# MLP's second projection: half of its work on columns 0 to 1023 as seven block products with 15 sums, in place of eight

## The chip, the cores and the metric

The kernel runs on one core of one Trainium2 chip. The metric is device time in microseconds (us), the median of several runs of one launch. A core has five engines, each with its own instruction stream: TensorE (PE: matmuls, and PEld for its weight loads), VectorE (DVE), ScalarE (ACT), GpSimd (POOL) and SyncE (SP), which here issues nearly all DMAs. Matmul results land in PSUM, which has 8 banks of 128 x 512 f32; everything else lives in SBUF.

## The reference

One layer of a streaming encoder on 256 tokens of width 2048, all in f32: a mixer (retention and gated delta rule), a cross-attention into 256 memory tokens, a squared-ReLU MLP and a final norm. What matters here is the last part:

```python
D_MODEL = 2048
SEQ = 256
D_FF = 4 * D_MODEL
...
        h = rms_norm(x, norm_ffn_g[l])
        x = x + jnp.square(jax.nn.relu(h @ w_ff1[l])) @ w_ff2[l]
    return rms_norm(x, norm_final_g)
```

`w_ff1` is 2048 x 8192 and `w_ff2` 8192 x 2048, 64 MB each.

## The kernel before

**Three matmuls for one product.** Each f32 operand is split into a rounded part ("hi", type fp32r) and the remainder ("lo"). A product is hi x hi + hi x lo + lo x hi: three matmuls into one PSUM bank.

**How a weight arrives.** `fetch` (L94) loads 512 x 512 weights (1 MB) by one DMA into a `raw` tile of 128 x 2048, of which there are three. It cuts it into two halves of 128 x 1024. For each half ScalarE rounds it into a `whi` tile (L117), and VectorE takes the remainder into a `wlo` tile (L118). `whi` and `wlo` have three buffers each, so a half can be made ready when TensorE has finished the half three before it.

**The MLP.** The hidden width is worked in four quarters (`fb`, 2048 hidden rows each). In a quarter the first projection runs first: eight calls of `blocks` (L183), each of which makes 256 hidden rows for all 256 tokens with hidden rows on the partitions. `evac_h` squares the ReLU into `hs` (two 128-row blocks of 256 tokens) and splits it into `hid`, four quads of four 128-row blocks, hi and lo. Then the second projection runs over four column blocks of 512 (`n`), one call of `chunk` (L145) each: it fetches the four 512-row pieces `q` of the quarter's weights for these columns and adds 16 row blocks x 2 token halves x 3 matmuls of 512 columns into two banks, one per half of the tokens (`t`). `evac_o` adds each bank, times the row's squared norm factor, into the residual `res` (L1125). In the last quarter it also sums the squares and multiplies by the final gain; the very last chunk has its own evacuation (`evac_last`) and keeps half of its weights in a space of its own (`hold`), so that the end is short.

**Banks.** `stream_ps` hands out a pair of banks (`s0`, `s1`) of which there are two pairs; `bank` hands out one of four others (`b`).

**Order.** The order of each engine's instructions is fixed when the program is built, by a planner that takes what is ready by a priority: the place in the program, moved ahead by 100000 places for a fetch with its rounding (`high_priority(offset=100000)`) and by 50000 for the evacuations. On the chip each engine then keeps to this order and waits where an operand or a buffer is late.

**Around the MLP.** `rt` (128 x 16 x 256) holds the residual in feature order until VectorE has transposed it blockwise into `tr`, of the same size (L1094). During the first projection of quarter 0, `place` (L1096) moves `tr` into the token-order residual `res` by 32 DMAs of 64 KB on SP. After that neither `rt` nor `tr` is used.

Of the kernel before, what the change touches and what calls it, by code (L numbers as in the profile page):

```python
# [10 lines left out]
F32 = mybir.dt.float32  # L11
F32R = mybir.dt.float32r
# [40 lines left out]
def trunk(ctx: ExitStack, tc: tile.TileContext, x_f, mem_f, positions, lead_f, small_f, w_in, ret_gn_g, w_out, w_xq,  # L53
# [213 lines left out]
    def square_sum(acc, src):  # L267
        junk = sm.tile([P, 512], F32, name="junk", tag="junk", bufs=1)
        act.activation(junk[:, :src.shape[1]], src, AF.Square, accum_out=acc)
# [831 lines left out]
                nc.sync.dma_start(to, tr[32 * a:32 * a + 32, :, b8 * 32:b8 * 32 + 32])  # L1101

    ssq4 = cp.tile([P, NT, 5], F32, name="ssq4")
    for fb in range(4):
        hid = []
        for b2 in range(8):
            hs = fp.tile([P, 2, S], F32, name="hs", tag="hs", bufs=2)
            if b2 % 2 == 0:
                hid.append(quad_a())

            def evac_h(b, ps):
                vec.scalar_tensor_tensor(hs[:, b, :], ps, 0.0, ps, op0=ALU.max, op1=ALU.mult)  # L1112
                qh, ql = (a[:, b2 % 2 * 2 + b, :] for a in hid[-1])
                act.activation(qh, hs[:, b, :], AF.Copy)
                vec.tensor_sub(ql, hs[:, b, :], qh.bitcast(F32))  # L1115

            blocks(h3, w_ff1[0], fb * D + b2 * 256, 2, evac_h)
            if fb == 0:
                place(b2)
        for n in range(4):  # L1120
            ns = slice(n * 512, (n + 1) * 512)

            def add(t, ps, c0, c1):
                got = res[:, t, n * 512 + c0:n * 512 + c1]
                vec.scalar_tensor_tensor(got, ps, rstd3q[:, t:t + 1], got, op0=ALU.mult, op1=ALU.add)  # L1125
                return got

            def evac_o(t, ps, c0, c1):
                got = add(t, ps, 0, 512)
                if fb == 3:  # L1130
                    square_sum(ssq4[:, t, n:n + 1], got)
                    vec.tensor_mul(got, got, gfin[:, ns])

            def evac_last(t, ps, c0, c1):
                got = add(t, ps, c0, c1)
                acc = ssq4[:, t, 4 if c0 else 3:5 if c0 else 4]
                if t == 0:
                    square_sum(acc, got)
# [16 lines left out]
                for c in (0, 3, 1, 2):  # L1155
# [7 lines left out]
                        act.activation(o, o, AF.Copy, scale=r)  # L1163
                    (act if t and c in (3, 2) else nc.sync).dma_start(out[0, t * P:(t + 1) * P, cs], o)

            last = fb == 3 and n == 3
            sums = []
            chunk(hid, cols(w_ff2[0, fb * D:(fb + 1) * D, :], n * 512), evac_last if last else evac_o,
                  hold=quad_b if last else None)


# [40 lines left out]
```

## Time and profile before

| | |
|---|---|
| time, median of 3 runs | 2066.89 us (2066.78 to 2068.17) |
| the profiled execution's own time | 2066.57 us |
| its span (first to last instruction) | 2064.8 us |
| granted TensorE clock, mean | 0.999 |
| DMA | 405.24 MB, mean 196 GB/s |
| MLP in the span | about 1360 to 2054 us |

The profile is of one execution, on the hardware. A page has busy times by engine, a chain of waits followed back from the last instruction, and groups of instructions by line and shape ("out<-in, partitions x elements"), with the mean duration and the idle time of the engine just before them and what ended it. Other views give the waits by pair, the instructions in order of time, or the busy time in chosen stretches. TensorE's matmuls overlap and their ends are modelled, so its busy time doesn't give its rate; the distance between starts does.

### The profile page before, as it was taken

Reading aid. Unit: us, or ns where it says so; the run is one execution under the profiler, and the core shown is the slowest. Engines: PE = TensorE matmul, PEld = TensorE weight load, DVE = VectorE, ACT = ScalarE, POOL = GpSimd, SP = SyncE. Lnnn points to the kernel's source line nnn. Section 1 sums busy time; section 2 is a strip of 40 time slices with the busy share of each in tenths; the row PEclk is TensorE's granted clock in tenths of the full one; section 3 lists DMA queues with packets and bytes.
Section 4 is the critical chain, followed back from the end, with each engine's and each line's share of the span. In section 5 each row is a group of like instructions: output and inputs, shape, how many; then the busy total and the mean of one; then the engine's idle time right before and its main releaser. Section 6 shows DMA issues by size and latency. Waiting matters only on the chain.

```text
span 2064.8 us, 28349 instructions
## 1 busy us (share of the span) xinstructions
PE 2054.2 (99%) x10922; PEld 1769.7 (86%) x10922; DVE 1412.2 (68%) x2249; ACT 1096.4 (53%) x1787; POOL 37.4 (2%) x50
## 2 busy tenths in 40 slices
PE   9999999999999999999999999999999999999998
PEld 7888888988888888888888898888888888888887
DVE  5887788778667975887567665776556556655655
ACT  5655764575457555755455555554344434434444
POOL 0000000000000000000000000000000000000000
PEclk9999999999999999999999999999999999999999
DMA  9689556565555655565577664678566566656654
GB/s 326 205 256 301 183 186 195 157 193 187 175 184 184 190 191 165 180 195 177 163 228 226 188 183 136 202 203 231 199 188 194 189 194 193 187 201 186 197 189 143
DMA packets 329224, 405.24 MB, mean 196 GB/s; under 512 B 34928, under 2 KB 239360, under 8 KB 328960
## 3 DMA queue, kind: packets, MB, share of 16 engines
q1 hardware_dynamic: 328656, 402.74, 62.4%
q8 instruction: 85, 1.39, 0.3%
q10 hardware_dynamic: 432, 0.69, 0.1%
q14 instruction: 51, 0.42, 0.1%
HBM read 389.74 MB, written 11.55 MB: 194 GB/s over the span
## 4 chain that ended last, share of the span: by engine, by line
PE 98%; DMA 1%; DVE 0%; issue 0%; ACT 0%; SPq 0%; POOLq 0%; POOL 0%; ACTq 0%; DVEq 0%
PE s L200 34%; PE s L201 18%; PE s L159 13%; PE s L160 13%; PE s L158 13%; DMA raw<-w_xkv 1%; PE b L779 1%; PE b L682 1%; PE b L130 1%; PE b L812 1%; PE b L129 1%; PE b L131 1%; PE s L385 0%; PE b L684 0%; PE s L386 0%; PE s L384 0%
## 5 line engine op out<-in xcount | busy, mean ns | idle before, releaser
L118 DVE TENSOR_TENSOR wlo<-raw,whi 128x1024 fp32r<-128x1024 f32 x696 | 850.7, 1223 | 493.3 <-ACT whi L117 484.0
L117 ACT ACTIVATE whi<-raw 128x1024 fp32r<-128x1024 f32 x696 | 737.4, 1060 | 701.3 <-PE s L160 355.6
L200 PE MATMUL s<-q,whi 128*128 128x512 f32 x3072 | 1059.1, 391 | 1.3 <-DVE q L126 1.3
L201 PE MATMUL s<-q,wlo 128*128 128x256 f32 x3072 | 836.8, 281 | 0.0
L200 PEld LDWEIGHTS s<-q,whi 128*128 128x128 f32 x3072 | 566.8, 188 | 112.4 <-DVE q L126 1.5
L201 PEld LDWEIGHTS s<-q,wlo 128*128 128x128 f32 x3072 | 576.9, 188 | 13.9 <-DVE wlo L118 0.4
L159 PE MATMUL s<-wlo,q 128*128 128x512 f32 (+1 forms) x1200 | 469.8, 391 | 0.0
L160 PE MATMUL s<-whi,q 128*128 128x512 f32 (+1 forms) x1200 | 467.4, 390 | 0.0
L158 PE MATMUL s<-whi,q 128*128 128x512 f32 (+1 forms) x1200 | 428.0, 390 | 0.0
L158 PEld LDWEIGHTS s<-whi,q 128*128 128x128 f32 x1200 | 225.2, 188 | 46.8
L160 PEld LDWEIGHTS s<-whi,q 128*128 128x128 f32 x1200 | 225.4, 188 | 45.7
L159 PEld LDWEIGHTS s<-wlo,q 128*128 128x128 f32 x1200 | 225.4, 188 | 45.4
L207 ACT ACTIVATE bo<-s 128x256 f32<-128x256 f32 x192 | 73.2, 381 | 112.9 <-PE s L201 112.8
L208 DVE TENSOR_TENSOR bo<-bo,s 128x256 f32<-128x256 f32 x192 | 80.0, 417 | 55.3 <-ACT bo L207 55.0
L641 DVE SCALAR_TENSOR_TENSOR acc<-bo,small,acc 128x255 f32<-128x255 f32 (+1 forms) x144 | 65.3, 480 | 1.8 <-ACT acc L638 0.6
L748 DVE TENSOR_TENSOR pr<-lw,tw 32x31 f32<-32x31 f32 (+15 forms) x124 | 40.4, 326 | 7.8 <-DMA lw<-scr_l 5.8
L750 DVE TENSOR_TENSOR tw<-tw,pr 32x31 f32<-32x31 f32 (+15 forms) x124 | 40.6, 328 | 2.1
L1125 DVE SCALAR_TENSOR_TENSOR res<-s,rstd3q,res 128x512 f32<-128x512 f32 (+1 forms) x32 | 22.3, 735 | 11.4 <-PE s L160 11.4
L638 ACT ACTIVATE acc<-bo,small 128x256 f32<-128x256 f32 x48 | 24.7, 514 | 7.7 <-DVE bo L208 7.6
L913 ACT ACTIVATE gth<-s 128x512 f32<-128x512 f32 x32 | 18.9, 590 | 16.8 <-PE s L160 12.6
L1112 DVE SCALAR_TENSOR_TENSOR hs<-bo 128x256 f32<-128x256 f32 x64 | 26.9, 422 | 1.1
L1115 DVE TENSOR_TENSOR q<-hs,q 128x256 fp32r<-128x256 f32 x64 | 26.7, 418 | 0.0
(309 smaller groups left out, 1170.7 us busy)
## 6 DMA issues: line engine op xcount, KB each, us to landing
raw<-w_in SPq DMA_DIRECT2D x143, 1024.0 KB
raw<-w_ff SPq DMA_DIRECT2D x128, 1024.0 KB
raw<-w_xkv SPq DMA_DIRECT2D x29, 1024.0 KB
raw<-w_out SPq DMA_DIRECT2D x16, 1024.0 KB
raw<-w_xq SPq DMA_DIRECT2D x16, 1024.0 KB
raw<-w_xo SPq DMA_DIRECT2D x16, 1024.0 KB
dec_d<-dec_w SPq DMA_DIRECT2D x8, 384.0 KB
dec<-dec_d SPq DMA_DIRECT2D x8, 384.0 KB
```

The source lines that it names most:

```text
L117: latest["hi"] = act.activation(hi[:, cs], src[:, cs], AF.Copy).ins
L118: latest["lo"] = vec.tensor_sub(lo[:, cs], src[:, cs], hi[:, cs].bitcast(F32)).ins
L158: pe.matmul(o, xh, wh, start=first, stop=False)
L159: pe.matmul(o, xh, wl, start=False, stop=False)
L160: pe.matmul(o, xl, wh, start=False, stop=last)
L200: pe.matmul(ps[b], lh, xhl, start=kk == 0, stop=False)
L201: pe.matmul(ps[b][:, :S], ll, xh, start=False, stop=kk == KT - 1)
L207: act.activation(o, ps[b][:, S:], AF.Copy)
L208: vec.tensor_add(o, o, ps[b][:, :S])
L641: vec.scalar_tensor_tensor(acc[:, d:], ps[:, :S - d], cw[:, j, blk:blk + 1], acc[:, d:], op0=ALU.mult, op1=ALU.add)
L748: vec.tensor_mul(pv, lw[:, j, j + 1:32].unsqueeze(2).to_broadcast([32, n, j + 1]), tw[:, j, 0:j + 1].unsqueeze(1).to_broadcast([32, n, j + ...
L750: vec.tensor_sub(tw[:, j + 1:32, 0:j + 1], tw[:, j + 1:32, 0:j + 1], pv)
```

## The change

Columns 0 to 1023 and the first 1024 hidden rows of each quarter are computed otherwise; the other 1024 rows of these columns, and columns 1024 to 2047, are computed as before. The hidden rows are taken as 128-row blocks in pairs, even and odd. With the token halves t0, t1 and the columns 0 to 511 and 512 to 1023 this makes a 2 x 2 block product: a11 and a12 are the even and odd hidden blocks of t0, a21 and a22 those of t1; b11 and b12 are the even weight blocks of the two column halves, b21 and b22 the odd ones. Eight block products become seven:

| product | goes to (column half, token half) |
|---|---|
| a11 b11 | `shared`, then (0, t0) |
| S1 (b12 - b11), S1 = a21 + a22 | `p5`, then (1, t0) and (1, t1) |
| S4 b22, S4 = a12 - S2 | the bank of (1, t0) |
| + S2 (b22 - b12 + b11), S2 = S1 - a11 | `shared` (on top of the first), then (1, t0) |
| a12 b21 | the bank of (0, t0) |
| + S3 (b22 - b12), S3 = a11 - a21 | `shared` (on top of both), then (0, t1) and (1, t1) |
| a22 (b21 - b22 + b12 - b11) | the bank of (0, t1) |

The four sums of the hidden are made and split by `token_sums`, called from `evac_h` for the first four of the eight blocks of the first projection. The four sums of the weights are made in place by VectorE in `form`, then rounded as a fetch is. The weight blocks are loaded by `load_block` into the spaces of `rt` and `tr`, 1 MB each. `seven` interleaves the products with the ordinary pieces (`plain`) of column blocks 2, 0 and 1, and uses all eight banks; column block 3 remains a `chunk`.

```diff
+    def add(n, t, ps, c0=0, c1=512):
+        got = res[:, t, n * 512 + c0:n * 512 + c1]
+        with tc.high_priority(offset=50000):
+            vec.scalar_tensor_tensor(got, ps, rstd3q[:, t:t + 1], got, op0=ALU.mult, op1=ALU.add)
+        return got
+
+    def finish_sum(n, t, ps, fb):
+        got = add(n, t, ps)
+        if fb == 3:
+            square_sum(ssq4[:, t, n:n + 1], got)
+            vec.tensor_mul(got, got, gfin[:, n * 512:(n + 1) * 512])
+
+    s_hl = tuple(fp.tile([P, 4, 512], F32R, name="s" + e, tag="s" + e, bufs=1) for e in "hl")
+    b11, b12, b22, b21 = (a[:, c:c + 8, :].rearrange("p k s -> p (k s)") for a in (rt, tr) for c in (0, 8))
+
+    def token_sums(i, hs):
+
+        sv = fp.tile([P, 4, P], F32, name="sv", tag="sv", bufs=1)
+        (a11, a21), (a12, a22) = ((hs[:, b, 0:P], hs[:, b, P:S]) for b in range(2))
+        vec.tensor_add(sv[:, 0], a21, a22)
+        vec.tensor_sub(sv[:, 1], sv[:, 0], a11)
+        vec.tensor_sub(sv[:, 2], a11, a21)
+        vec.tensor_sub(sv[:, 3], a12, sv[:, 1])
+        split([a[:, i, :] for a in s_hl], sv.rearrange("p a s -> p (a s)"))
+
+    def load_block(to, rows, which, n):
+
+        src = rows[0:D // 2, n * 512:(n + 1) * 512].rearrange("(i two p) n -> p i two n", two=2, p=P)[:, :, which, :]
+        with tc.high_priority(offset=100000):
+            fetched.append(nc.sync.dma_start(to.rearrange("p (i n) -> p i n", i=4), src).ins)
+
+    def seven(fb, hid, rows):
+
+
+        own = [stream_ps() for _ in range(2)]
+        shared, p5 = bank(), bank()
+        own.append([bank(), bank()])
+        opened = set()
+
+        def triple(o, lhs, rhs, last=False):
+            for j, (l, r) in enumerate(((0, 0), (0, 1), (1, 0))):
+                pe.matmul(o, lhs[l], rhs[r], start=id(o) not in opened, stop=last and j == 2, skip_group_check=True)
+                opened.add(id(o))
...
+        def form(raw, minus=None):
+            got = []
+            with tc.high_priority(offset=100000):
+                for c in range(2):
+                    src = raw[:, c * 1024:(c + 1) * 1024]
+                    if minus is not None:
+                        vec.tensor_sub(src, *(a[:, c * 1024:(c + 1) * 1024] for a in minus))
+                    hi, lo = (wp.tile([P, 1024 + room], F32R, name=nm, tag=nm, bufs=3)[:, :1024]
+                              for nm, room in (("whi", 64), ("wlo", 0)))
+                    latest["hi"] = act.activation(hi, src, AF.Copy).ins
+                    latest["lo"] = vec.tensor_sub(lo, src, hi.bitcast(F32)).ins
+                    got.append((hi.rearrange("p (k n) -> p k n", n=512), lo.rearrange("p (k n) -> p k n", n=512)))
+            return got
+
+        def product(o, lhs, halves, last=True):
+            for i in range(4):
+                triple(o, lhs(i), [a[:, i % 2, :] for a in halves[i // 2]], last=last and i == 3)
...
+        plain(2, 0)
+        load_block(b22, rows, 1, 1)
+        product(shared, part(0, 0), form(b11))
+        add(0, 0, shared)
+        plain(2, 1)
+        load_block(b21, rows, 1, 0)
+        product(p5, summed(0), form(b11, (b12, b11)))
+        add(1, 0, p5)
+        add(1, 1, p5)
+        plain(0, 2)
+        product(own[1][0], summed(3), form(b22), last=False)
+        plain(2, 2)
+        product(shared, summed(1), form(b11, (b22, b11)))
+        add(1, 0, shared)
+        plain(0, 3)
+        product(own[0][0], part(1, 0), form(b21), last=False)
+        finish_sum(0, 0, own[0][0], fb)
+        plain(2, 3)
+        for t in range(NT):
+            finish_sum(2, t, own[2][t], fb)
+        product(shared, summed(2), form(b12, (b22, b12)))
+        add(0, 1, shared)
+        add(1, 1, shared)
+        plain(1, 2)
+        product(own[0][1], part(1, 1), form(b11, (b21, b11)), last=False)
+        finish_sum(0, 1, own[0][1], fb)
+        plain(1, 3)
+        for t in range(NT):
+            finish_sum(1, t, own[1][t], fb)
+
     for fb in range(4):
         hid = []
+        rows = w_ff2[0, fb * D:(fb + 1) * D, :]
...
+                if b2 < 4 and b:
+                    token_sums(b2, hs)
 
             blocks(h3, w_ff1[0], fb * D + b2 * 256, 2, evac_h)
+            if b2 > 5:
+                load_block((b11, b12)[b2 - 6], rows, 0, b2 - 6)
             if fb == 0:
                 place(b2)
-        for n in range(4):
+        seven(fb, hid, rows)
+        for n in range(3, 4):
```

`plain(n, q)` fetches one 512 x 512 piece and runs its 24 matmuls into the two banks of column block `n`; `part` and `summed` pick the hidden block or the sum that is the stationary operand.

More of the change, by code (lines that the diff above doesn't have):

```diff
@@ L1164, in evac_last @@
                     (act if t and c in (3, 2) else nc.sync).dma_start(out[0, t * P:(t + 1) * P, cs], o)
-            last = fb == 3 and n == 3
+            last = fb == 3
             sums = []
-            chunk(hid, cols(w_ff2[0, fb * D:(fb + 1) * D, :], n * 512), evac_last if last else evac_o,
+            chunk(hid, cols(rows, n * 512), evac_last if last else evac_o,
                   hold=quad_b if last else None)
```

21 lines of the change are left out of this document (12 added, 9 removed).

## The prediction

> **What bounds the kernel now.** I read the page from the top: span and busy times, then the chain of waits, then the list of who waited for whom on TensorE.
>
> ```profile
> span 2064.8 us, 28349 instructions
> ...
> PE 2054.2 (99%) x10922; PEld 1769.7 (86%) x10922; DVE 1412.2 (68%) x2249; ACT 1096.4 (53%) x1787; POOL 37.4 (2%) x50
> ...
> PE 98%; DMA 1%; DVE 0%; issue 0%; ACT 0%; SPq 0%; POOLq 0%; POOL 0%; ACTq 0%; DVEq 0%
> ```
>
> ```profile
> PE s L200 <- DVE q L126: 1.3, 1, 1.3
> PE b L242 <- DVE warm L238: 1.1, 1, 1.1
> PE s L384 <- DVE q L319: 0.5, 1, 0.5
> PE s L385 <- DVE wlo L118: 0.2, 1, 0.2
> ```
>
> The second fence is TensorE's whole list of waits (total us, times, longest): 3.1 us in the kernel, none of them on the MLP's lines L158 to L160. So a matmul taken out there comes off the end, as long as TensorE goes on finding its operands ready. Busy time says little about that pace, since matmuls overlap; the pace has to come from when things start. In the second projection one half of a fetched weight (128x1024) feeds 12 matmuls of 512 columns, and ScalarE's next rounding is released when TensorE has finished a half:
>
> ```profile
> 1481.48 1.06 ACT L117 ACTIVATE whi<-raw 128x1024 fp32r<-128x1024 f32 x1 [1.66 <-PE s L160]
> 1484.20 1.06 ACT L117 ACTIVATE whi<-raw 128x1024 fp32r<-128x1024 f32 x1 [1.66 <-PE s L160]
> 1486.92 1.06 ACT L117 ACTIVATE whi<-raw 128x1024 fp32r<-128x1024 f32 x1 [1.66 <-PE s L160]
> ```
>
> ```profile
> 1486.43 1.40 DVE L1125 SCALAR_TENSOR_TENSOR res<-s,rstd3q,res 128x512 f32<-128x512 f32 x2
> 1488.01 1.23 DVE L118 TENSOR_TENSOR wlo<-raw,whi 128x1024 fp32r<-128x1024 f32 x1 [0.18 <-ACT whi L117]
> ```
>
> ```profile
> 1486.72 0.62 PE L158 MATMUL s<-whi,q 128*128 128x512 f32 x2
> ```
>
> The starts lie 2.72 us apart (1484.20 less 1481.48), so a matmul costs 2.72 / 12 = 0.2267 us. The last three rows give the price of making a half ready: TensorE goes on to the next half at 1486.72; the buffer of the finished one is rounded from 1486.92 and its remainder taken from 1488.01 to 1489.24. That is 2.52 us, for a buffer needed two halves (5.44 us) later: 2.9 us to spare. The three views of TensorE, ScalarE and VectorE agree that the two helpers wait for TensorE here.
>
> By stretches (columns: busy us of PE, PEld, DVE, ACT, POOL, then clock, DMA share, GB/s) a second projection is 1443 to 1530 or 1618 to 1705, and a first projection lies between:
>
> ```profile
> 1443.00:1530.00 87.00, 87.00 (x385) 72.04 (x385) 45.33 (x45) 35.11 (x36) 0.00 (x0) 1.00 0.60 194
> 1530.00:1618.00 88.00, 88.00 (x511) 77.90 (x510) 55.62 (x77) 42.00 (x60) 0.00 (x0) 1.00 0.63 191
> 1618.00:1705.00 87.00, 87.00 (x387) 72.05 (x386) 45.21 (x45) 35.11 (x36) 0.00 (x0) 1.00 0.60 193
> ```
>
> VectorE is half idle (45 of 87 us) where the change puts its sums, and the granted clock is 1.00.
>
> **What goes.** For columns 0 to 1023 and the first 1024 rows of each quarter, before has 2 column blocks x 2 fetches x 4 row blocks x 2 token halves x 3 matmuls = 96; after has 7 products x 4 x 3 = 84. Twelve fewer in each of four quarters: 48 x 0.2267 = 10.9 us. All are 128x512 forms, so the price needs no other row.
>
> The Trainium skill, "TensorE: Matmul & The Clock Gate", in the section on the 56 ns gap, puts a warm matmul at N / 2.4 GHz plus about 2.5 ns, 215.7 ns for 512 columns; by that the saving would be an estimated 10.4 us. Here the pace is 226.7 ns, and I keep the row.
>
> **What comes: rounding, sums and adds in the second projection.** The costs of one are in these groups (last columns: busy us, mean ns, then idle before):
>
> ```profile
> L118 DVE TENSOR_TENSOR wlo<-raw,whi 128x1024 fp32r<-128x1024 f32 x696 | 850.7, 1223 | 493.3 <-ACT whi L117 484.0
> L117 ACT ACTIVATE whi<-raw 128x1024 fp32r<-128x1024 f32 x696 | 737.4, 1060 | 701.3 <-PE s L160 355.6
> ```
>
> Per quarter, the seven products round 14 halves where there were 8 (6 more on ScalarE, 6 more on VectorE), four of the products form their weight operand with two 128x1024 differences each (8 more on VectorE, of the form and size of L118: 1.223 us), and 6 more results of 128x512 are added into the residual (0.70 each, two in 1.40). VectorE gets 14 x 1.223 + 6 x 0.70 = 21.3 us, ScalarE 6 x 1.06 = 6.4 us.
>
> How dense is that? The new stretch holds 8 ordinary fetches of 5.44 us and 7 products of 2.72 us: 62.6 us of TensorE. VectorE has there 30 remainders and 8 differences (46.5 us) and 12 adds (8.4 us): 54.9 us, 88%. ScalarE has 30 x 1.06 = 31.8 us, 51%. Neither becomes the bound by its total, and every product stands between two ordinary fetches. But a product eats its two halves twice as fast, 6 matmuls or 1.36 us each, while there are still three buffers. The half after a product takes the buffer freed by the half before it: it is needed 2.72 us later and costs 2.52 us to make. The 2.9 us to spare are 0.2 us there, and 0.43 us for the remainder, which only the second matmul reads. The second half of a product has 4.08 less 2.52, 1.6 us. So seven times a quarter, 28 times in all, TensorE waits if VectorE is in the middle of something else when the remainder's turn comes. Other work than remainders is 8 x 1.223 + 12 x 0.70 = 18.2 us of 62.6, so 29% of the time; what is then left of an operation is about half of its mean 0.91 us, less what is to spare: some 0.3 us. 28 x 0.29 x 0.3 = 2.4 us; I take 2.5. The bounds are nothing (every difference done early, for its blocks are loaded long before) and a whole difference each time, 28 x 1.22 = 34 us. I stand near the low end, because the adds at 1486.43 went into the gap ahead of the remainder at 1488.01, which shows an order that fills gaps.
>
> **What comes in the first projection: token sums.** Four times a quarter, four 128x128 sums and one 128x512 split. Nearest rows: 285 ns for a 128x128 operation with a PSUM operand, 418 for a 128x256 sum in SBUF, and a 128x512 split.
>
> ```profile
> L1115 DVE TENSOR_TENSOR q<-hs,q 128x256 fp32r<-128x256 f32 x64 | 26.7, 418 | 0.0
> ...
> L688 DVE SCALAR_TENSOR_TENSOR dj<-b,ident 128x128 f32<-128x128 f32 x32 | 8.0, 285 | 0.0
> ...
> L126 DVE TENSOR_TENSOR q<-xn,q 128x512 fp32r<-128x512 f32 x8 | 5.3, 682 | 0.0
> ...
> L125 ACT ACTIVATE q<-xn 128x512 fp32r<-128x512 f32 x8 | 4.7, 624 | 0.2 <-DVE xn L489 0.2
> ```
>
> Between 4 x 0.285 + 0.682 = 1.8 and 4 x 0.418 + 0.682 = 2.4 us of VectorE, so 7.3 to 9.4 us a quarter on top of 55.6 of 88, and 2.5 us on ScalarE. VectorE's idle 32 us hide it, and the spare 2.9 us of each half outlast one burst: nothing. Were that cover gone, 16 bursts x 1.8 would be 29 us.
>
> **What moves.** Four fetches of 1 MB a quarter become four block loads of 1 MB, into the spaces of `rt` and `tr` instead of the three `raw` buffers; bytes and their 2 KB pieces are the same, SP issues as many. At a DMA share of 0.60 there is room in quarters 1 to 3, and the three raw buffers now cover only the ordinary fetches, so these come earlier against their use. Quarter 0 is the second rival. The product banks are safe: `shared` is written again 21.8 and then 13.6 us of matmuls after its add could begin, and the last chunk needs a bank pair whose add has an ordinary fetch (5.44 us) of cover. TensorE's order keeps twelve or twenty-four matmuls between dependent steps, so no wait is added there; all of this at nothing.
>
> **The sum.** The profiled execution took 2066.57 us, 1.8 outside the span; the median shown is 0.3 above it. 2066.57 - 10.9 + 2.5 = 2058.2, and on the median's footing 2058.5 us.
>
> **Rivals.** *All hidden.* The differences run ahead while remainders wait for ScalarE, and nothing is lost: 2066.9 - 10.9 = 2056.0. For it: VectorE's 484 us of waiting on L117. Against it: 0.2 us to spare.
>
> *The block loads starve quarter 0.* The loads of `b11` and `b12` carry the fetches' priority but wait for no raw buffer, only for `rt` to be free; they can go out as soon as `rt` is transposed, into the stretch where the small placing DMAs fill the queues:
>
> ```profile
> 1364.95 0.37 SPq L104 DMA_DIRECT2D raw<-w_ff  x1
> 1369.55 3.96 SPq L1101 DMA_DIRECT2D res<-tr  x5
> ```
>
> ```profile
> 1395.25 2.24 ACT L117 ACTIVATE whi<-raw 128x1024 fp32r<-128x1024 f32 x2 [2.98 <-DMA raw<-w_ff]
> ```
>
> ```profile
> 1381.00:1468.00 87.00, 87.00 (x472) 75.63 (x471) 53.88 (x71) 40.23 (x57) 0.00 (x0) 1.00 0.82 218
> ```
>
> There a fetch was already late by 2.98 us with TensorE unharmed. Two more MB at 218 GB/s are 9.6 us; less the sliver of cover that is left (2.9 spare less the part used, 1.5 or so) 8 us reach the end: 2058.5 + 8 = 2066.5, no change. Against it: the DMA engines are not full (0.82), and three buffers hold 16 us of work.
>
> *The differences stand in the remainders' way, and it is slower.* VectorE works in the order written when the program is built. If that order has the pair of differences of the next product (or of two, since `b12` and `b11` are free together) ahead of the remainder TensorE needs next, each difference costs 1.22 us at a place with 0.2 us to spare. It has happened on a small scale in the mixer, where a remainder whose rounding ended at 233.34 began at 234.47, behind two later products:
>
> ```profile
> 232.28 1.06 ACT L117 ACTIVATE whi<-raw 128x1024 fp32r<-128x1024 f32 x1 [1.41 <-PE s L200]
> ```
>
> ```profile
> 233.41 0.74 DVE L702 SCALAR_TENSOR_TENSOR alt<-b,sc,dec 128x512 f32<-128x512 f32 x1
> 234.07 0.48 DVE L705 SCALAR_TENSOR_TENSOR alt<-b,sc,dec 128x256 f32<-128x256 f32 x1
> 234.47 1.22 DVE L118 TENSOR_TENSOR wlo<-raw,whi 128x1024 fp32r<-128x1024 f32 x1
> ```
>
> There 2.9 us to spare swallowed it. Of the 32 differences, 9 on the path (10.9 / 1.22) use up the gain; with 16 the time is 2066.9 - 10.9 + 19.5 = 2075.5, with 12 it is 2070.6. The Trainium skill, "PSUM — Partial Sum Buffer", section on engine and sequencer instructions, says that VectorE's queue is strictly first in, first out, so a remainder can't pass what stands before it; those three rows agree. Against this rival: the blocks are there early and the sums need no buffer.
>
> **Chances.** Forecast, with waits of 1 to 6.5 us: 0.42, time 2057 to 2062.5. All hidden: 0.23. Starved quarter 0, or waits that just eat the gain: 0.12. Differences in the way: 0.23. About 0.2% or 4.1 us is what a measurement can tell from no change; the first two cases are faster by more (0.65), the third is within it (0.12), the last is slower (0.23). The range: down to 2055.3 (all hidden, less the spread of the runs), up to 2071.5, which takes in the starved case and the milder half of the last one; the likeliest case's own range stands above.
>
> **What would show it.** TensorE with 10874 matmuls, and each second projection at 87.0 - 2.7 us plus its waits; new rows in TensorE's list of waits, on L118's successor (remainders), at most 0.7 us each and just after products. VectorE up by 24 x 1.223 + 32 x 1.223 + 24 x 0.74 + 29 to 38, to about 1530 us; ScalarE by 24 x 1.06 + 16 x 0.62, to about 1130. Wrong would be: waits over 1 us with a difference just ended on VectorE (third rival), waits before 1450 us that go back to a weight DMA (second), no waits at all (first), a difference that takes clearly more than 1.22 us, or a pace other than 0.2267 us in the products.

## The result and the profile after

The changed kernel takes 2078.63 us (median of 6 runs, 2077.86 to 2080.48), the kernel before on the same chip 2067.14 us (6 runs, 2066.58 to 2068.17): ratio 1.0056, 95% interval 1.0045 to 1.0066. It is slower by some 11.5 us, where 8.4 us less were forecast, and outside the forecast's range.

The page of the changed kernel, busy times and the chain that ended last:

```profile
span 2077.2 us, 28457 instructions
...
PE 2053.2 (99%) x10874; PEld 1763.4 (85%) x10874; DVE 1512.1 (73%) x2409; ACT 1130.8 (54%) x1827; POOL 37.5 (2%) x50
...
PE 94%; DMA 2%; ACT 2%; DVE 1%; SPq 1%; issue 1%; POOLq 0%; POOL 0%; ACTq 0%
```

The work is what was forecast: 48 matmuls fewer, VectorE 1512 us (about 1530 forecast), ScalarE 1131 (about 1130). But the chain, 98% TensorE before, now runs through transfers, their issue, ScalarE and VectorE for 6% of its length. TensorE's list of waits over the MLP of the changed kernel (total us, times, longest) has five new entries; before there was none:

```profile
PE s L1146 <- ACT whi L1165: 4.6, 5, 1.8
PE b L1146 <- ACT whi L1165: 2.8, 4, 0.7
PE s L200 <- ACT whi L117: 2.6, 3, 1.9
PE s L201 <- DVE wlo L118: 2.2, 4, 0.6
PE s L1146 <- ACT whi L117: 0.9, 1, 0.9
```

Where they lie is seen by cutting both traces at the first matmul of each projection (in quarter 0, at the first one behind the norm's sums, 54 matmuls into the first projection). Columns: stretch, its length, then busy us of PE, PEld, DVE, ACT, POOL, granted clock, DMA share, GB/s. The kernel before: the first projection of quarter 0, the second one of quarter 1, the second one of quarter 3 up to the end of the last matmul:

```profile
1363.86:1443.17 79.31, 79.31 (x460) 70.03 (x460) 54.82 (x77) 38.14 (x57) 0.70 (x1) 1.00 0.91 227
...
1618.54:1705.61 87.07, 87.07 (x386) 72.08 (x385) 45.58 (x45) 34.96 (x36) 0.00 (x0) 1.00 0.60 193
...
1969.27:2057.19 87.92, 87.92 (x434) 74.47 (x432) 48.78 (x57) 39.59 (x52) 0.55 (x1) 1.00 0.48 159
```

The same three stretches of the changed kernel:

```profile
1365.56:1453.21 87.65, 82.81 (x460) 71.06 (x460) 59.47 (x97) 40.15 (x61) 0.70 (x1) 0.98 0.97 254
...
1627.88:1714.22 86.34, 84.95 (x375) 69.68 (x373) 64.83 (x65) 41.50 (x42) 0.00 (x0) 1.00 0.60 195
...
1977.24:2069.52 92.28, 88.25 (x422) 73.05 (x420) 68.18 (x77) 45.95 (x58) 0.55 (x1) 0.98 0.33 107
```

So there are three separate losses. The first projection of quarter 0, which has the same matmuls, grew by 8.34 us. The second projections of quarters 0 to 2 fell by only 0.73 to 0.75 us each, though twelve matmuls less are 2.72. The last one grew by 4.36. Together 8.34 - 3 x 0.74 + 4.36 = 10.5. The spans differ by 12.4: another 1.7 us stand ahead of the MLP (its start at 1365.56 instead of 1363.86), in code that the change does not touch; in the runs below this start lies anywhere from 1363.3 to 1366.1, so it is the spread of single executions.

### The profile page after: what moved, and what is told of

The parts are those of the page before. It is cut to its first block, busy times and chain, and to the rows that moved or that the text cites. A ratio compares the mean times of both kernels' runs of the same rounds, so it can differ in the third digit from the quotient of the medians.

```text
span 2077.2 us, 28457 instructions
## 1 busy us (share of the span) xinstructions
PE 2053.2 (99%) x10874; PEld 1763.4 (85%) x10874; DVE 1512.1 (73%) x2409; ACT 1130.8 (54%) x1827; POOL 37.5 (2%) x50
## 4 chain that ended last, share of the span: by engine, by line
PE 94%; DMA 2%; ACT 2%; DVE 1%; SPq 1%; issue 1%; POOLq 0%; POOL 0%; ACTq 0%
PE s L200 32%; PE s L201 16%; PE s L159 9%; PE s L160 9%; PE s L158 9%; PE b L1146 6%; PE s L1146 6%; DMA raw<-w_ff 1%; SPq L1101 1%; PE s L384 1%; PE s L385 1%; PE s L386 1%; PE b L779 1%; PE b L130 1%; PE b L812 1%
## 5 line engine op out<-in xcount | busy, mean ns | idle before, releaser
L118 DVE TENSOR_TENSOR wlo<-raw,whi 128x1024 fp32r<-128x1024 f32 x664 | 809.6, 1223 | 391.0 <-ACT whi L117 384.9
L117 ACT ACTIVATE whi<-raw 128x1024 fp32r<-128x1024 f32 x664 | 703.8, 1060 | 613.8 <-PE s L200 240.3
L159 PE MATMUL s<-wlo,q 128*128 128x512 f32 x816 | 320.4, 393 | 0.0
L160 PE MATMUL s<-whi,q 128*128 128x512 f32 x816 | 318.0, 390 | 0.0
L158 PE MATMUL s<-whi,q 128*128 128x512 f32 x816 | 294.0, 390 | 0.0
L158 PEld LDWEIGHTS s<-whi,q 128*128 128x128 f32 x816 | 153.1, 188 | 31.9
L159 PEld LDWEIGHTS s<-wlo,q 128*128 128x128 f32 x816 | 153.4, 188 | 30.7
L160 PEld LDWEIGHTS s<-whi,q 128*128 128x128 f32 x816 | 153.3, 188 | 30.7
L1146 PE MATMUL s<-whi,q 128*128 128x512 f32 x320 | 102.1, 394 | 2.6 <-ACT whi L1165 1.8
L1146 PE MATMUL b<-whi,q 128*128 128x512 f32 x288 | 90.7, 389 | 0.0
L1146 PEld LDWEIGHTS s<-whi,q 128*128 128x128 f32 x320 | 60.8, 190 | 16.2 <-ACT whi L1165 2.2
L1146 PEld LDWEIGHTS b<-whi,q 128*128 128x128 f32 x288 | 54.1, 188 | 11.4
L1146 PE MATMUL s<-wlo,q 128*128 128x512 f32 x160 | 63.1, 394 | 0.0
L1165 ACT ACTIVATE whi<-rt 128x1024 fp32r<-128x1024 f32 x40 | 42.5, 1061 | 37.6 <-PE b L1146 30.3
L1146 PE MATMUL b<-wlo,q 128*128 128x512 f32 x144 | 56.1, 390 | 0.0
```

The lines of the kernel that those rows point to most:

```text
L117: latest["hi"] = act.activation(hi[:, cs], src[:, cs], AF.Copy).ins
L118: latest["lo"] = vec.tensor_sub(lo[:, cs], src[:, cs], hi[:, cs].bitcast(F32)).ins
L158: pe.matmul(o, xh, wh, start=first, stop=False)
L159: pe.matmul(o, xh, wl, start=False, stop=False)
L160: pe.matmul(o, xl, wh, start=False, stop=last)
L1146: pe.matmul(o, lhs[l], rhs[r], start=id(o) not in opened, stop=last and j == 2, skip_group_check=True)
```

## The experiments

Times below are medians with the ratio to the kernel before on the same chip; the kernels ran on several chips, on which the kernel before took 2067.0 to 2067.8 us, so a difference of less than 1 us between two of them says nothing. "Second projection" lengths go from the first matmul to the next projection's first, or for the last quarter to the end of the last matmul. "Gaps" are distances from row to row of TensorE's timeline less 0.2267 us for each matmul in the row (0.118 for the 256-column ones), where over 0.3 us. A row can hold several matmuls, so some that run at a lower clock count as a gap too: 1.0 us or so of the largest sums below.

### Quarter 0: the block loads

In the changed kernel SyncE issued both loads for `rt` first, ahead of the placing transfers and of nearly all weights of this projection, and those for `tr` much later (1422.31):

```profile
1366.65 0.37 SPq L104 DMA_DIRECT2D raw<-w_ff  x1
1369.00 2.62 SPq L1134 DMA_DIRECT2D rt<-w_ff  x2
1371.66 6.93 SPq L1101 DMA_DIRECT2D res<-tr  x4
1378.69 2.30 SPq L104 DMA_DIRECT2D raw<-w_ff  x1
```

ScalarE's waits between 1355 and 1446 and TensorE's longest gap there, in the same kernel:

```profile
ACT whi L117 <- DMA raw<-w_ff: 25.9, 8, 4.7
```

```profile
1404.21 0.73 PE L200 MATMUL s<-q,whi 128*128 128x512 f32 x2 [1.94 <-ACT whi L117]
...
1405.47 0.79 PE L201 MATMUL s<-q,wlo 128*128 128x256 f32 x2 [0.53 <-DVE wlo L118]
```

The rounding waits eight times for a weight's transfer (25.9 us; once, 3.0 us, before), and TensorE after it. The experiment only moves the loads of this quarter:

```diff
     def load_block(to, rows, which, n):
...
-        with tc.high_priority(offset=100000):
+        with ExitStack() as order:
+            if first_quarter[0]:
+                order.enter_context(tc.issue_after(fetched[-1]))
+            order.enter_context(tc.high_priority(offset=100000))
             fetched.append(nc.sync.dma_start(...).ins)
```

> In quarter 0 alone, the loads of the blocks are issued behind the weight transfers that the program has asked for so far, not ahead of them. Theory (the block loads stand ahead of the weights of the first projection and starve it): the first projection of quarter 0 falls from 87.65 us to between 79.3 and 80.5, the rounding's waits for a raw buffer's transfer fall from 25.9 us in the stretch 1355 to 1445 to about 5, and the whole takes 8 us less, about 2070.5. Rival (the token sums or the small placing transfers by themselves make the stretch longer): it stays at 87 or so and the time at 2078.6. Second rival (the megabytes are only moved and now starve the second projection of quarter 0): the first projection gets its 8 us back, the second one loses several.

Measured: 2069.59 us, ratio 1.0012 (1.0003 to 1.0021), 9.0 less than the changed kernel. Its first projection of quarter 0, and ScalarE's waits for these transfers:

```profile
1365.45:1444.82 79.37, 79.37 (x460) 70.03 (x460) 60.30 (x97) 40.39 (x61) 0.70 (x1) 1.00 0.99 257
```

```profile
ACT whi L117 <- DMA raw<-w_ff: 6.6, 4, 2.2
```

79.37 us against 79.31 before, with all token sums in it (VectorE 60.3 us against 54.8) and as many bytes a second as in the changed kernel (257 and 254 GB/s): it was the order of the transfers on SyncE's queue, neither the sums nor the megabytes. The second rival falls as well, since the next second projection stayed at 86.33. The DMA engines were busy for 0.99 of that stretch and TensorE still found its weights.

### Quarters 0 to 2: what makes the two gaps

In each second projection of the changed kernel TensorE stands twice for 0.86 us. The first place in quarter 1, TensorE and then VectorE:

```profile
1635.84 0.84 PE L1146 MATMUL b<-whi,q 128*128 128x512 f32 x3
1637.37 0.50 PE L1146 MATMUL b<-whi,sh 128*128 128x512 f32 x1 [0.69 <-ACT whi L1165]
1637.71 0.39 PE L1146 MATMUL b<-wlo,q 128*128 128x512 f32 x1
```

```profile
1633.52 1.22 DVE L1162 TENSOR_TENSOR rt<-tr,rt 128x1024 f32<-128x1024 f32 x1
1634.65 0.42 DVE L1222 TENSOR_TENSOR q<-hs,q 128x256 fp32r<-128x256 f32 x1
1634.99 1.22 DVE L1162 TENSOR_TENSOR rt<-rt 128x1024 f32<-128x1024 f32 x1
1636.12 2.36 DVE L118 TENSOR_TENSOR wlo<-raw,whi 128x1024 fp32r<-128x1024 f32 x2
```

By the list the wait is for a product's rounding: the matmul that waits takes a token sum `sh`, and it stands in TensorE's order in the middle of an ordinary piece, which goes on at 1637.71. But VectorE has two differences (L1162) ahead of the piece's remainders (L118, from 1636.12), so the second suspect is VectorE. Two runs part them, one that ties TensorE's order and one that ties the differences:

```diff
         def plain(n, q):
...
+            with in_turn():          # the same around the matmuls of product()
                 for i in range(4):
...
+        def in_turn():
+            return tc.issue_after(done[0]) if done[0] is not None else ExitStack()
```

> TensorE's order is tied: no piece of a second projection (ordinary piece or product) may have a matmul ahead of the last matmul of the piece before it. Theory A (two first matmuls of products are written ahead of the rest of an ordinary piece, and TensorE stands 0.86 us at each for a rounding): both gaps of each quarter go, 8 x 0.86 = 6.9 us, the time is about 2072. Rival B (the differences stand ahead of the remainders on VectorE, and TensorE would have waited for the remainder anyway): the first gap of each quarter stays at 0.7 to 0.9 us, now at a remainder, the second falls to 0.3, so 2 to 3 us in all, about 2076.

```diff
         def form(raw, minus=None):
-            got = []
+            got, ahead = [], latest["lo"]
...
-                        vec.tensor_sub(src, *(...))
+                        with tc.issue_after(ahead):
+                            vec.tensor_sub(src, *(...))
```

> Each product's weight differences are put behind the last remainder written before them in VectorE's order. Theory A (TensorE's own order makes the two gaps of each quarter): the gaps stay at 0.86 us, the time at 2078.6 within 1. Rival B (differences ahead of remainders make them): the gaps shrink, 3 to 6 us in all, about 2074. A third outcome, if the differences now come late for the products that need them: new waits at roundings of the four products, up to 1.2 us each, and a longer time.

With TensorE's order tied: 2078.99 us, ratio 1.0057 (1.0042 to 1.0072), no gain. The first gap is still there and now names the remainder; the second has shrunk:

```profile
1637.26 0.50 PE L1147 MATMUL b<-wlo,q 128*128 128x512 f32 x1 [0.71 <-DVE wlo L118]
...
1645.87 0.50 PE L1147 MATMUL s<-wlo,q 128*128 128x512 f32 x1 [0.15 <-DVE wlo L118]
```

The second projection of quarter 1 falls by only 0.5 us, to 85.84, and the last quarter gives it back (93.92). With the differences behind the remainders: 2076.14 us, ratio 1.0045 (1.0030 to 1.0060), 2.5 less, a little under the 3 to 6 that were expected. Both gaps are gone; a smaller one appears once a quarter, at the remainder of a product that now follows two differences, and quarter 1 takes 85.40 us:

```profile
1680.48 1.40 DVE L1108 SCALAR_TENSOR_TENSOR res<-b,rstd3q,res 128x512 f32<-128x512 f32 x2
1681.81 2.35 DVE L1167 TENSOR_TENSOR wlo<-rt,whi 128x1024 fp32r<-128x1024 f32 x2
```

```profile
1683.08 0.50 PE L1146 MATMUL s<-wlo,q 128*128 128x512 f32 x1 [0.35 <-DVE wlo L1167]
```

So the differences ahead of remainders make the first gap and part of the second, whichever order TensorE has; tying TensorE's order takes some 0.5 us a quarter off the second. The second run alone doesn't clear TensorE's order, for there the planner no longer puts a token sum's matmul into the middle of an ordinary piece. The control takes the differences out (`if minus is not None and False`), so that four products multiply plain blocks:

> Leaves out the eight weight differences of each quarter (four products then multiply the plain blocks, so the output is another one); VectorE loses 9.8 us a quarter, nothing else changes. Theory (differences written ahead of remainders make the two gaps of each quarter, and VectorE has more than all of the time in the product stretch of the last quarter: 54.9 us that the prediction counted, and 4.7 us of held remainders and 4.1 us of closing multiplications that it did not count, 63.7 us beside 62.6 of TensorE): the second projections of quarters 0 to 2 fall from 86.3 to 84.6 or so, the last from 92.3 to 86 to 88, and the time to about 2068. Rival for the gaps (TensorE's own order): they stay, 86.3. Rival for the last quarter (the held halves' transfer comes late): it falls by no more than the 1.7 us of the gaps, to 90.5, and the time to 2072.

2068.46 us, ratio 1.0006 (0.9997 to 1.0015). Every second projection of quarters 0 to 2 is free of gaps, though in quarter 1 two matmuls with a token sum again stand in the middle of ordinary pieces (at 1634.27 and 1642.43): without the differences that order costs nothing.

```profile
1622.91:1707.27 84.36, 84.36 (x375) 69.83 (x374) 56.02 (x57) 41.41 (x42) 0.00 (x0) 1.00 0.60 200
```

87.07 - 84.36 = 2.71 us, the full price of twelve matmuls. The eight differences cost 86.34 - 84.36 = 1.98 us a quarter in the changed kernel. The last quarter fell to 89.01, less far than the 86 to 88 of the theory and further than the 90.5 of its rival; its rows are shown below.

Could an idle engine take them? GpSimd, with the block loads as in the first experiment (`pool.tensor_sub` in `form`):

> The block loads of quarter 0 go behind the weights as in e1_blocks_later (2069.6), and the weight differences are computed on GpSimd, which is idle here, not on VectorE. If GpSimd works beside VectorE without slowing it and takes less than some 8 us for one difference: the gaps of quarters 0 to 2 go (1.7 us each) and the last quarter loses 3 to 5 of its 92 us, so 2060 to 2062. If the two hinder each other where they read the same memory: the remainders take clearly more than 1.22 us while a difference runs, and the time stays at 2069 or goes above. If one difference takes over 10 us: the four products wait for it, and the time is longer than 2070.

2092.83 us, ratio 1.0127 (1.0111 to 1.0142), the slowest of all; quarter 1 took 92.08 us. GpSimd's and VectorE's rows:

```profile
1629.77 2.40 POOL L1167 TENSOR_TENSOR rt<-rt 128x1024 f32<-128x1024 f32 x1 [143.47 <-DVE wlo L1171]
1632.25 2.50 POOL L1167 TENSOR_TENSOR rt<-tr,rt 128x1024 f32<-128x1024 f32 x1
```

```profile
1629.88 2.57 DVE L1228 TENSOR_TENSOR q<-hs,q 128x256 fp32r<-128x256 f32 x1
1632.38 2.66 DVE L1225 SCALAR_TENSOR_TENSOR hs<-bo 128x256 f32<-128x256 f32 x1
```

An operation of 0.42 us on VectorE takes 2.57 and 2.66 us: each ends just behind the GpSimd operation beside it. The second outcome held: here the engines do not share, one stands while the other works, so a difference on GpSimd can cost VectorE 2.4 us, not 1.2.

### The last quarter

The changed kernel, ScalarE and TensorE. The rows `q<-raw` are the held halves of the last chunk:

```profile
2026.23 2.01 ACT L117 ACTIVATE q<-raw 128x1024 fp32r<-128x1024 f32 x2 [2.14 <-DMA raw<-w_ff]
2028.15 1.04 ACT L117 ACTIVATE whi<-raw 128x1024 fp32r<-128x1024 f32 x1
```

```profile
2029.24 0.73 PE L1146 MATMUL s<-whi,q 128*128 128x512 f32 x2 [0.87 <-ACT whi L117]
2031.74 0.50 PE L1146 MATMUL s<-whi,q 128*128 128x512 f32 x1 [1.77 <-ACT whi L1165]
```

It looks as if the held halves, waiting for their transfer, only stood in the way of the rounding at 2028.15. So they went behind the pieces before them, by the kernel's own helper:

```diff
-        held = {q: fetch(pieces_of(q), 4, 512, hold=hold) for q in ((2, 3) if hold else ())}
+        held = {}
+        if hold:
+            with behind():
+                held = {q: fetch(pieces_of(q), 4, 512, hold=hold) for q in (2, 3)}
```

> The held conversions for the last chunk of a quarter (two halves fetched ahead into buffers of their own) are put behind the hi, lo and raw work of the pieces before them in each engine's order. Theory (in the last quarter ScalarE stands at the held rounding that waits 2.14 us for its transfer, and the rounding that TensorE needs next stands behind it): the last second projection falls from 92.3 us by 4 to 5.4 us to 87 or 88, and the time to 2073.5 or so; nothing else changes. Rival (the last quarter is longer because VectorE is full there): it stays at 92, the time at 2078.6.

2078.16 us, ratio 1.0056 (1.0040 to 1.0073): nothing. The two gaps are gone, and as much comes a dozen us later, at the last chunk: all four held halves now stand in a row, and the rounding behind them waits 1.88 us for its own transfer (TensorE's rows in that kernel):

```profile
2041.74 0.62 PE L161 MATMUL s<-whi,q 128*128 128x512 f32 x2 [1.69 <-ACT whi L117]
...
2043.91 0.80 PE L162 MATMUL s<-wlo,q 128*128 128x512 f32 x1 [1.44 <-DVE wlo L118]
```

That place was no better. The kernel without differences says something more about these two gaps. It has 9.8 us less of VectorE in this stretch, and both gaps are there all the same, behind the same wait of ScalarE for a held half's transfer:

```profile
1968.31:2057.32 89.01, 86.32 (x422) 71.86 (x420) 59.20 (x69) 45.78 (x58) 0.55 (x1) 1.00 0.33 111
```

```profile
2015.37 2.01 ACT L117 ACTIVATE q<-raw 128x1024 fp32r<-128x1024 f32 x2 [2.18 <-DMA raw<-w_ff]
```

```profile
2018.37 0.73 PE L1146 MATMUL s<-whi,q 128*128 128x512 f32 x2 [0.91 <-ACT whi L117]
2020.88 0.50 PE L1146 MATMUL s<-whi,q 128*128 128x512 f32 x1 [1.77 <-ACT whi L1165]
```

So these 3 us follow the late transfer, and do not need the differences. With the differences tied (e4_differences_later) both gaps are gone, but the quarter is as long: TensorE now waits for remainders (1.63, 0.57 and 1.82 us). The other suspect is therefore the amount of VectorE's work: in the last quarter the product stretch also holds four held remainders and six multiplications by the closing gain (L1115), which no other quarter has. Three runs take work away there, all with the edits of e1_blocks_later and e4_differences_later: the multiplications on GpSimd (`pool.tensor_mul` in `finish_sum`), left out (the output then lacks this gain), and nothing held (`hold=None`):

> With the changes of e1_blocks_later and e4_differences_later (together 2078.6 - 9.0 - 2.5 = 2067.1 if they add up), the last quarter's six multiplications by the closing gain are done on GpSimd, not on VectorE: 4.1 us less for VectorE, all in the last quarter. Theory (VectorE's total there is above TensorE's): the last second projection falls by 2 to 4 us from 92, the time is 2063 to 2065. Rival (the held halves' late transfer sets it): unchanged, 2067.

> With the changes of e1_blocks_later and e4_differences_later, and the six multiplications by the closing gain in the last quarter left out (the output is another one): VectorE has 4.1 us less, some 2 of it at the end of the product stretch. Theory (VectorE is full at that end): the last second projection falls from 92.1 by 2 to 4 us, the time to 2063 to 2065. Rival (only the order matters: ScalarE stands at a held half whose transfer is late): it stays at 91 to 92, the time at 2067. On GpSimd the same six operations took 1.5 us off the projection, while remainders beside them took 1.87 and 2.28 us.

> With the changes of e1_blocks_later and e4_differences_later, and the last chunk converted piece by piece as in the other quarters, nothing held ahead: 4.7 us of VectorE and 4.2 us of ScalarE leave the end of the product stretch, and both rows of the last chunk are finished behind the last matmul. Theory (the held conversions are what is too much there): TensorE's gaps of over 0.3 us ahead of the last chunk, 6.2 us with e4_differences_later, go down to 1 or less; the closing work behind the last matmul grows by about 3 us (the first row's adds, squares and scalings); the time is about 2064. Rival (the products and closing multiplications alone are too much): gaps of 3 us or more stay, and the time is 2067 to 2070.

Three more, with the same two edits, leave the work and move the held pieces ahead:

```diff
+        def keep(q):
+            if fb == 3:
+                with behind():        # not in g1_held_earlier
+                    held[q] = fetch(cols(rows, 1536)(q), 4, 512, hold=quad_b)
...
         add(1, 1, p5)
+        keep(2)                       # i2_held_in_middle: each one product later
         plain(0, 2)
         product(own[1][0], summed(3), form(b22), last=False)
+        keep(3)
```

> With the changes of e1_blocks_later and e4_differences_later (2067.1 if they add up), the two held pieces of the last chunk are fetched and converted behind the second and the third product of the last quarter, not behind the seventh: 4.7 us of VectorE and 4.2 us of ScalarE move from the end of the product stretch to its first half. Theory (the end of the stretch, about 22 us of TensorE, has 22.8 us of VectorE work, because the held remainders and the closing multiplications fall there; in the first half there is room): the last second projection falls from 92.1 to between 85.5 and 88, the time to 2061 to 2063. Rival (VectorE is full over the whole product stretch of that quarter): the waits move ahead with the conversions, the projection stays above 90 and the time above 2065.

> As g1_held_earlier, but the two held pieces, fetched behind the second and the third product of the last quarter, are also tied behind the roundings and remainders written before them, so that they cannot move ahead into the end of the first projection as they did there (from 1965 us on). Theory (the work fits if it lies where VectorE has room): the gaps go from 3.9 us to 1 or less, the last second projection takes 86 to 87.5 us, the time is 2060 to 2062. Rival (VectorE has too much work in this quarter, wherever it lies): 3 us of gaps or more stay, now elsewhere, the projection stays above 88 and the time above 2063.

> As i1_held_in_place, but one product later: the held pieces behind the third and the fourth product. Theory (place decides): gaps of 1 us or less at one of the two placings, 2060 to 2062. Rival (amount decides): both placings keep gaps of about 3 us, and differ only in where they stand; above 2063.

Measured; the last three columns are of the profiled execution, whose own time stands beside the median:

| kernel | median, ratio to before (interval) | own time | last second projection | gaps in it |
|---|---|---|---|---|
| changed | 2078.63, 1.0056 (1.0045 to 1.0066) | 2078.89 | 92.28 | 5.8 |
| e4_differences_later | 2076.14, 1.0045 (1.0030 to 1.0060) | 2076.81 | 92.38 | 6.2 |
| f3_closing_gpsimd | 2066.00, 0.9995 (0.9986 to 1.0004) | 2064.47 | 90.57 | 4.8 |
| g2_no_closing_gain | 2062.91, 0.9981 (0.9972 to 0.9991) | 2062.59 | 88.88 | 2.9 |
| h2_no_hold | 2065.00, 0.9989 (0.9980 to 0.9999) | 2065.10 | 86.90 | 1.9 |
| g1_held_earlier | 2063.70, 0.9987 (0.9978 to 0.9995) | 2066.42 | 91.35 | 3.9 |
| i1_held_in_place | 2064.28, 0.9983 (0.9974 to 0.9992) | 2065.31 | 89.26 | 3.1 |
| i2_held_in_middle | 2063.45, 0.9978 (0.9969 to 0.9988) | 2063.82 | 88.92 | 2.9 |

Amount counts: 4.1 us less of VectorE take 3.5 us off the projection (g2, against e4; up to 1.7 of it is the granted clock, 0.92 over 22 us there and 1.00 here). With nothing held it is the shortest, but the work behind its last matmul grows from 7.7 us to 11.6, and the 1.9 us of gaps that stay lie between what the theory (1 or less) and its rival (3 or more) expected. On GpSimd the same multiplications took some 2 us each, and two of VectorE's remainders beside them 1.87 and 2.28 us in place of 1.22; of the 3.5 us only 1.8 were gained. Place counts too: moved ahead, the held pieces cost 3.1 and 3.5 us less, the clock among it (i1, i2, against e4; the profiled execution of g1 is the slowest of its 11 runs, with a granted clock of 0.86 from 1978 to 1990, and says little). But at neither place do the gaps go below 2.9 us: the rival's sign for "amount". The stretch of 22 us in which they lie, in the kernel before with its held halves, with e4_differences_later, and with the held pieces in the middle:

```profile
2009.00:2031.00 22.00, 22.00 (x99) 18.22 (x98) 15.65 (x16) 12.68 (x15) 0.00 (x0) 1.00 0.69 236
```

```profile
2019.00:2041.00 22.00, 17.68 (x67) 12.78 (x66) 22.00 (x25) 14.35 (x20) 0.00 (x0) 0.92 0.46 161
```

```profile
2008.00:2030.00 22.00, 20.38 (x89) 15.99 (x88) 21.66 (x24) 12.84 (x18) 0.00 (x0) 1.00 0.30 96
```

VectorE (the third busy time, behind PE and PEld) rises from 15.65 to 22.00 of 22 us while TensorE falls to 17.68; with the held pieces elsewhere it is still 21.66. So with the differences behind the remainders the end of the last quarter is bound by VectorE: products and closing multiplications by themselves leave gaps of 1.9 us (h2), and the held pieces on top cost another 3 us or so. How the 5 us of the changed kernel itself divide between the late transfer and VectorE's amount is not parted by these runs.

### What is better than both

The last quarter as eight products, since seven took longer there, with the two cures for the other quarters:

```diff
-        seven(fb, hid, rows)
-        for n in range(3, 4):
+        if fb < 3:
+            seven(fb, hid, rows)
+        for n in range(3 if fb < 3 else 0, 4):
```

(with no token sums and block loads in that quarter, and `last = fb == 3 and n == 3`)

> With the changes of e1_blocks_later and e4_differences_later, and the last quarter multiplied with eight products as in the kernel before (no block loads, no token sums there). The last second projection then takes 87.9 us as before, not 92.3 (or 89.6, without its two gaps): 2067.1 - 4 = 2063, below the 2067.1 of the kernel before. If it is not below 2065, the loss of the last quarter does not come from the seven products in it.

2062.43 us, ratio 0.9977 (0.9968 to 0.9987): 4.8 less than the kernel before on that chip (2067.23), as 3 x (87.07 - 85.39) = 5.0 says. Seven products in the last quarter too, with the held pieces in the middle (i2), come to the same within the intervals: there the last projection takes 88.92 us, with eight 87.92. Its first projection of quarter 0, a second projection and the last one:

```profile
1364.94:1444.31 79.37, 79.37 (x461) 70.03 (x460) 60.40 (x97) 40.38 (x61) 0.70 (x1) 1.00 0.99 260
1618.06:1703.45 85.39, 84.94 (x375) 69.67 (x373) 64.82 (x65) 41.36 (x42) 0.00 (x0) 1.00 0.58 197
1965.47:2053.39 87.92, 87.92 (x434) 74.48 (x432) 48.76 (x57) 39.82 (x52) 0.55 (x1) 1.00 0.47 160
```

To get the last 1.0 us a quarter, one difference was tied behind the first remainder of the piece before it and one behind the second (a list `lows` of the fetched pieces' remainders, `ahead = lows[-2:]`, `ahead[c]`):

> As f4_last_quarter_eight (2062.4: blocks of quarter 0 behind the weights, eight products in the last quarter), but a product's first difference is tied behind the first remainder of the ordinary piece before it and its second difference behind the second one, not both behind the second. With both behind the second, a second projection took 85.4 us, without differences 84.4. Theory (the 1.0 us left is the product's own halves coming late behind two differences): 84.4 to 84.9, three quarters, the time 2060 to 2061. Rival (the first difference now delays the ordinary piece's second remainder, as in the changed kernel): 85.4 to 86.3, the time 2062.4 to 2065.

2062.21 us, ratio 0.9975 (0.9966 to 0.9985): no difference that these runs can tell. A second projection takes 85.16 us instead of 85.39, and the gap at the product's remainder is still 0.5 us.

## Why the prediction was wrong

**Right.** The price of what goes: 48 x 0.2267, which the kernel without differences shows as 2.71 us a quarter. The price of a difference, 1.22 us (L1162 above), and the work of each engine. Token sums at nothing: 79.37 us with them, 79.31 without. No wait appeared at the product banks.

**The step that failed first: "What moves", "all of this at nothing".** The load moves were written down as free, with quarter 0 left to a rival of 12% and 8 us. The rival was right in mechanism, and in size (8.34 us, and 9.0 less in the run that undoes it) partly by luck: it counted the time of two MB, but with the loads behind the weights as many bytes cost nothing, and some 1.7 of the 8.34 us are a granted clock of 0.98, which it did not have. Against it stood that the DMA engines were not full and that three buffers hold 16 us. Neither was the point: the block loads need no `raw` buffer, so the fetches' priority put them at once ahead of the placing transfers and the next weights, and these came late though the total fitted. The row of before that showed a fetch late by 2.98 us should have been given the larger chance.

**The waits, 2.5 us in all, were mis-sized.** Quarters 0 to 2 lost 1.98 us each, not 0.6. The term took it for chance whether VectorE is in the middle of something (0.29 x 0.3 us). It isn't chance: the planner's order is fixed, and it puts differences ahead of the ordinary piece's remainders at the same places of each quarter (the gaps of quarters 0 to 2 end 9.5 and 18.65 us behind the start of each second projection). That is the third rival at a scale of 1.6 differences a quarter (1.98 / 1.22). That no wait is added in "TensorE's order" holds only while operands are in time: tying it took some 0.5 us a quarter off the changed kernel, and without differences it cost nothing. The sign given for these waits misled too: they were to show at remainders, and in the changed kernel TensorE's list names roundings.

**The four quarters were taken to be alike.** "Neither becomes the bound by its total" rested on 54.9 us of VectorE in 62.6. In the last quarter four held remainders (4.7 us) and six closing multiplications (6 x 0.69 = 4.1) stand there too, 63.7 us in all. That quarter cost 92.28 - (87.92 - 2.72) = 7.1 us, of which 2.0 are the differences as in the other quarters and 5.1 the last quarter's own. The count of VectorE explains only a part: without any difference 89.01 - 85.20 = 3.8 us of the 7.1 stayed, 3 of them the two gaps behind a held half whose transfer came late, and no run parts the two causes in the changed kernel itself. With the differences behind the remainders, some 3.5 us went when the held pieces stood elsewhere (92.38 to 88.92, the clock among it), the rest did not. No rival had this quarter.

**The sum as it was:** -10.9 for the matmuls, +8.3 for quarter 0, +7.9 (4 x 1.98) for the differences and +5.1 for the last quarter's own loss, 10.4 us; the median rose by 11.5, and the 1.1 us between them are no more than the spread of single executions. The likeliest time, the sign and the range all missed, because the cases were treated as alternatives: the second rival, a piece of the third and an unlisted one all came true together.

## What to carry to other kernels

A transfer that had no buffer to wait for went out as early as its priority allowed: when a load is moved to a free space, look at what its queue now issues later. Count an engine's work in each repetition of a loop by itself, the last one above all: what was done only there was 8.8 us of VectorE here, where 7.7 of 62.6 were free. And where an engine is nearly full (VectorE 88% here), look at the order on its queue instead of taking a wait for chance: the rows of one repetition gave it for all three that are alike.

## What was not expected of the hardware

**Short gaps cost twice, but not always.** Behind the gaps in quarter 0 and in the last quarter the granted clock drops for a few us. The changed kernel, two stretches of 6 us, and its matmuls in the second:

```profile
1405.00:1411.00 6.00, 5.53 (x23) 4.90 (x24) 2.96 (x6) 2.03 (x4) 0.00 (x0) 0.72 1.13 226
2032.00:2038.00 6.00, 6.00 (x19) 4.63 (x19) 5.84 (x7) 3.26 (x5) 0.00 (x0) 0.72 0.84 295
```

```profile
2035.12 1.48 PE L1146 MATMUL s<-whi,q 128*128 128x512 f32 x3
2036.40 0.63 PE L1146 MATMUL s<-wlo,q 128*128 128x512 f32 x1
```

Three matmuls in 1.28 us are 0.43 each, nearly twice 0.2267; 6 x 0.28 = 1.7 us are lost each time. With the same two gaps of 1.0 and 2.05 us the kernel without differences shows 1.00 there. The Trainium skill, "TensorE: Matmul & The Clock Gate", section "What's actually happening", says that the clock is decided over a free-running window of about 3.4 us, which would explain why the same gap is punished in one execution and not in another; it asks for an idle window, and in the changed kernel no single gap was longer than 2.1 us.

**GpSimd and VectorE exclude each other in these operations.** The rows with 2.57 and 2.66 us for an operation of 0.42 us are above. An add that takes one input from PSUM was not lengthened: in f3_closing_gpsimd L1108, at 2011.60, took 0.75 us beside a multiplication of 2.18 us on GpSimd. The Trainium skill, "SBUF — State Buffer", section "Who interferes with whom", says that a VectorE instruction with two SBUF inputs contends with a GpSimd instruction that reads SBUF, and that the shared pair of ports is an exclusive lock; both rows agree (the second takes `bo` as both of its inputs).
